# Gates of a routed layer by one 256-column matmul per token, with other portions of side work per block

## The chip, the cores and the metric

One of the cores of a Trainium2 chip runs the program. The metric is the device time of one execution in microseconds (us).

## What is computed

The reference is one layer of a decoder with 512 tokens of width 2048. Attention comes first (latent heads and sliding-window heads, and an output projection that is added to the input: `h`). What matters here is the last part, a retrieval over 16384 small experts, `h + peer(rms_norm(h))`:

```
q = (xt @ w_q).reshape(T, PEER_HEADS, 2, PEER_DQ // 2)
s = jnp.einsum('thpd,hpnd->thpn', q, sub_keys)
s_half, i_half = lax.top_k(s, PEER_TOPK)
...
top_s, pos = lax.top_k(cand, PEER_TOPK)
idx = jnp.take_along_axis(cand_idx, pos, axis=-1)
g = jax.nn.softmax(top_s, axis=-1)
...
u = expert_u[ic]
a = jnp.einsum('cd,ced->ce', xc, u)
w = (gc * jax.nn.gelu(a)).astype(xc.dtype)
return jnp.einsum('ce,ced->cd', w, expert_v[ic])
```

Each token picks 8 x 16 = 128 experts out of 128 x 128. An expert is one row of `expert_u` and one row of `expert_v`, both 16384 x 2048 float32 (134 MB each).

## The kernel before, in words

The kernel does the last part in two ways. For tokens 128 to 511 (the dense tokens, `TD` = 384) it multiplies with all experts and weights the result with a gate that is zero for experts not picked. For tokens 0 to 127 it gathers the picked rows, one row per token and slot.

**U stage.** `u_block(e)` (line 875) takes 128 experts: `u_turn` (line 862) transposes their rows on VectorE and `split` (line 116) makes a high part on ScalarE (line 117) and a low part on VectorE (line 118), three half blocks ahead of their use. TensorE then does 48 matmuls with 384 columns (lines 883 to 885). ScalarE applies the activation function (line 890), and GpSimd's queue writes the tile to `acts_d` in memory (line 891). There are 128 such blocks.

**V stage.** From line 1055 on, 16 groups of 4 column ranges load rows of `expert_v`, split them (line 118), and TensorE multiplies them (lines 191 to 193) with the weighted activations, which `w_block` (line 1033) makes on GpSimd from the activations (`wg`, from `acts_d`) and the gates (`gg`, from `gates_d`). VectorE adds the sums to the tokens' rows (line 1059).

**Side work and what orders it.** Three things are spread over these blocks by generators that give back a cost after each piece. A `Filler` (line 122) has a credit; `run(budget)` adds the budget, up to 4.0 in all, and takes pieces while the credit is above zero. The order is that of the program; the scheduler at compile time may move an instruction ahead when its engine is free and its operands are there. On each engine the order is fixed then.

- *Routing* (`route`, line 756): the top-16 searches of one projection tile, some 10 cost units each, on VectorE and GpSimd. They start in the projection before the U stage. The loop of line 990 runs U blocks with two portions of 1.4 each until no routing is left. Only then does the program queue the next two.
- *Gates* (`dense_gates`, line 899): three times 0.6 for the tables, and then 0.17 for each of 384 tokens (and 7 more steps, as sums lag 7 tokens behind). `expand` makes for a token a one-hot tile `oj` of the 128 slots' second indices (GpSimd, line 907), a one-hot tile `on` of the first (VectorE, line 909), and `oi`, that tile times the slots' weights, once with the high and once with the low part of the weights (ScalarE, line 912). `merge` multiplies `oj` with both parts of `oi`, each 128 columns, and accumulates them in one 128-column range of a PSUM bank (line 922). After four tokens the bank is full, and ScalarE copies it to `stage` (line 929). After 16 tokens ScalarE's queue writes `stage` to `gates_d` (line 932). The share per half block is 36/(124 - e), e being the number of routing blocks.
- *Gathered rows* (`gathered`, line 956): 256 steps of 2.3 units, 128 with rows of `expert_u` (a dot product on VectorE, line 973) and 128 with rows of `expert_v` (scaled and added on VectorE, line 976). Each row tile of 1.05 MB is fetched by an indirect transfer from GpSimd's queue (line 965), two steps ahead into three buffers. In the U stage each half block gives them 0.85 (line 1020), in the V stage each of the 256 steps 1.6 (line 1067). What is left then runs in a drain after the last matmul.

Of the kernel before, what the change touches and what calls it, by code (L numbers as in the profile page):

```python
# [15 lines left out]
AF = mybir.ActivationFunctionType  # L16
ALU = mybir.AluOpType
# [19 lines left out]
SG = 8  # L37
NSG = NK // SG
GT = 16
# [13 lines left out]
def block_kernel(ctx, tc, x, positions, norm1_gain, w_in, q_a_gain, w_q_b, kv_a_gain, w_kv_b, mla_q_gain,  # L53
                 mla_k_gain, swa_q_gain, swa_k_gain, swa_sinks, rel_bias_table, group_out_gain, w_out,
                 norm2_gain, peer_w_q, peer_sub_keys, peer_u, peer_v, out):
    nc = tc.nc
# [10 lines left out]
    def pool(name, bufs=1, side=None, stack=ctx, **kw):  # L67
        return stack.enter_context(tc.tile_pool(name=name, bufs=bufs, side=side, reuse_waits="tile", **kw))
# [7 lines left out]
    def acc_tile(name="acc"):  # L76
        return psum.tile([128, 512], F32, name=name, tag="acc", bufs=5)

    def tp_tile(name="tp"):
        return psum.tile([128, 512], F32, name=name, tag="tp", bufs=3)  # L80
# [35 lines left out]
    def split(hi, lo, src):  # L116
        first[0] = nc.scalar.activation(hi, src, AF.Copy)  # L117
        mark[0] = nc.vector.tensor_tensor(lo, src, hi.bitcast(F32), op=ALU.subtract)  # L118
# [33 lines left out]
    def flush(n=None):  # L152
        for _ in range(len(later) if n is None else min(n, len(later))):
            later.pop(0)()
# [486 lines left out]
    for k in range(len(units) + 3):  # L641
        if k < len(units):
# [3 lines left out]
            pieces, i, n = filling[k]  # L646
# [157 lines left out]
    def weigh(t, dst):  # L804
        e = exs[t]
        nc.scalar.activation(e, e, AF.Exp)
        z = small.tile([128, PH], F32, name="gz")
        nc.vector.tensor_reduce(z, e, axis=AX.X, op=ALU.add)
        rz = small.tile([128, PH], F32, name="grz")
        nc.vector.reciprocal(rz, z)  # L810
        nc.vector.tensor_tensor(dst.rearrange("p (h s) -> p h s", h=PH), e,
                                rz[:, :, None].to_broadcast([128, PH, TOPK]), op=ALU.mult)
# [49 lines left out]
    def u_turn(n):  # L862
        if n >= 2 * NK:
            return
        e, hf = divmod(n, 2)
        if hf == 0:
            u_load(e + 2)
        hi, lo = part_pair(n, [128, 8, 128])
        uT = up.tile([128, 8, 128], F32, name="uT")
        nc.vector.transpose(uT.rearrange("p k (b j) -> p b k j", j=32),  # L870
                            u_raw[e].rearrange("p b (k i) -> p b k i", k=KC)[:, :, hf * 8:hf * 8 + 8, :])
        split(hi, lo, uT)
        u_parts[n] = hi, lo

    def u_block(e, budget, pace=0.0):
        pa = acc_tile("pa")
        for hf in range(2):
            n = 2 * e + hf
            u_turn(n + 3)
            hi, lo = u_parts.pop(n)  # L880
            for k in range(8):
                kk = hf * 8 + k
                nc.tensor.matmul(pa[:, :TD], hi[:, k, :], xTd[0][:, kk, :], start=kk == 0, stop=False)  # L883
                nc.tensor.matmul(pa[:, :TD], hi[:, k, :], xTd[1][:, kk, :], start=False, stop=False)  # L884
                nc.tensor.matmul(pa[:, :TD], lo[:, k, :], xTd[0][:, kk, :], start=False, stop=kk == KC - 1)  # L885
            filler.run(budget)
            gatherer.run(pace)
        ga = xtp.tile([128, TD], F32, name="ga", bufs=2)
        with tc.issue_after(first[0].ins):
            nc.scalar.activation(ga, pa[:, :TD], AF.Gelu_apprx_tanh)  # L890
        nc.gpsimd.dma_start(acts_d[e], ga)
# [7 lines left out]
    def dense_gates():  # L899
        slT = [gb.tile([128, TD], F32, name=f"slT{r}") for r in range(2)]  # L900
        gT = [gb.tile([128, TD], F32R, name=f"gT{r}") for r in range(2)]
        hot, banks, stages = {}, {}, {}
        LAG = 7

        def expand(t):
            oj = gb.tile([128, NK], F32R, name="oj", bufs=LAG + 2)
            nc.gpsimd.tensor_scalar(oj, iot, slT[1][:, t:t + 1], None, op0=ALU.is_equal)  # L907
            on = gb.tile([128, NK], BF16, name="on", bufs=4)
            nc.vector.tensor_scalar(on, iotb, slT[0][:, t:t + 1], None, op0=ALU.is_equal)
            oi = gb.tile([128, 2, NK], F32R, name="oi", bufs=LAG + 2)  # L910
            for r in range(2):
                nc.scalar.activation(oi[:, r, :], on, AF.Copy, scale=gT[r][:, t:t + 1].bitcast(F32))  # L912
            hot[t] = oj, oi

        def merge(t):
            oj, oi = hot.pop(t)
            i = t % 4
            if i == 0:
                banks[t // 4] = acc_tile("gps")
            gps = banks[t // 4]  # L920
            for r in range(2):
                nc.tensor.matmul(gps[:, i * 128:(i + 1) * 128], oj, oi[:, r, :], start=r == 0, stop=r == 1)  # L922
            if i < 3:
                return
            g0, tb = t // GT, t % GT - 3
            if tb == 0:
                stages[g0] = gb.tile([128, NSG, GT, SG], F32, name="stage", bufs=2)
            stage = stages[g0]
            nc.scalar.activation(stage[:, :, tb:tb + 4, :].rearrange("p g t e -> p t g e"),
                                 gps.rearrange("p (t g e) -> p t g e", t=4, e=SG), AF.Copy)  # L930
            if tb == GT - 4:
                nc.scalar.dma_start(
                    bass.AP(tensor=gates_d.tensor, offset=gates_d.offset + g0 * GT * SG,
                            ap=[[TD * SG, 128], [128 * TD * SG, NSG], [1, GT * SG]]),
                    stage.rearrange("p g t e -> p g (t e)"))

        for t in range(1, NT):
            ts = slice((t - 1) * 128, t * 128)
            gt = gb.tile([128, SLOTS], F32, name="gt")
            weigh(t, gt)  # L940
            tp = tp_tile()
            for r in range(2):
                nc.tensor.transpose(tp[:, r * 128:(r + 1) * 128], ijs[t][:, r].rearrange("p h s -> p (h s)"), ident)
            nc.tensor.transpose(tp[:, 256:384], gt, ident)
            for r in range(2):
                nc.scalar.activation(slT[r][:, ts], tp[:, r * 128:(r + 1) * 128], AF.Copy)
            split(gT[0][:, ts], gT[1][:, ts], tp[:, 256:384])
            yield 0.6
        for t in range(TD + LAG):
            if t < TD:  # L950
                expand(t)
            if t >= LAG:
                merge(t - LAG)
            yield 0.17
# [28 lines left out]
    gatherer = Filler(paced=True)  # L983
# [5 lines left out]
    e = 0  # L989
    while filler.queue or later:  # L990
        flush(4)
        u_block(e, 1.4)
        e += 1
    filler.add(settle())
    filler.add(first_tokens())
# [7 lines left out]
    share = 36.0 / (NK - 4 - e)  # L1003
    gts, wgs, wb = {}, {}, {}

    def gate_tile(g):
        if g < NSG:
            gg = wp.tile([128, TD, SG], F32, name="gg", bufs=2)
            nc.sync.dma_start(gg, gates_d[g].rearrange("j (t e) -> j t e", e=SG))
            gts[g] = gg  # L1010

    def act_tile(e):
        if e < NK:
            wgs[e] = wp.tile([128, TD], F32, name="wg", bufs=AHEAD)
            nc.sync.dma_start(wgs[e], acts_d[e])
# [1 line left out]
    AHEAD = 5  # L1017
    wp = None
    while e < NK:
        u_block(e, share, 0.85)  # L1020
        e += 1
        if not filler.queue and wp is None:
            stg.close()
            wp = pool("wp", side="right")
            gate_tile(0)
            for i in range(AHEAD):
                act_tile(i)
# [22 lines left out]
    for g in range(NSG):  # L1050
        for c in range(4):
            acc = [acc_tile(), acc_tile(), tp_tile()]
            for i, w in enumerate(weights(v_rows[g * SG * 128:(g + 1) * SG * 128], SG, c * 512, 512, turn=4 * g + c)):
                k0 = 2 * i
                for t in range(NT - 1):
                    products(acc[t], lambda hl, kk, t: wb[g * SG + kk][hl][:, t * 128:(t + 1) * 128], t, k0, SG, w, 512)
                    if k0 == SG - 2:
                        hc = h[t + 1][:, c * 512:(c + 1) * 512]
                        mark[0] = nc.vector.tensor_tensor(hc, acc[t], hc, op=ALU.add)
                        if g == NSG - 1:  # L1060
                            nc.sync.dma_start(out[(t + 1) * 128:(t + 2) * 128, c * 512:(c + 1) * 512], hc)
                nxt = (g + 1) * SG
                if c < 3 and k0 < 4:
                    w_block(nxt + 2 * c + k0 // 2)
                if c == 3 and k0 > 2:
                    w_block(nxt + 4 + k0 // 2)
                gatherer.run(1.6)
    gatherer.drain()


# [23 lines left out]
```

## Time and profile before

| | us |
|---|---|
| median of 3 runs | 3233.54 (3232.82 to 3234.42) |
| the profiled execution, its own time | 3233.09 |
| its span, first to last instruction | 3231.4 |
| TensorE busy | 3104.4 (96%) |
| VectorE busy | 2367.1 (73%) |
| ScalarE busy | 1271.4 (39%) |
| GpSimd busy | 1248.2 (39%) |

The mean granted clock of TensorE is 0.983 of full speed. The DMA engines move 731.74 MB. The profile calls TensorE PE (its weight loads PEld), VectorE DVE, ScalarE ACT, GpSimd POOL and SyncE SP. Matmuls are pipelined: the duration of one is longer than the step to the next, so steps are read from their starts. The same holds to a smaller degree for VectorE, where the busy time of a stretch is less than the sum of durations.

### The profile page before, as it was taken

To read this page: it belongs to the slowest core of one execution; us is meant where nothing else is said; L and a number is where in the kernel's file an instruction comes from. 1 tells how busy PE (TensorE), PEld (TensorE's weight loads), DVE (VectorE), ACT (ScalarE), POOL (GpSimd) and SP (SyncE) were. 2 spreads that over 40 slices of the span, in tenths; PEclk is the share of its full clock that TensorE was granted. 3 is DMA by queue.
4 is the path that set the end of the run, shared out by engine and by line. 5 is a ranking of instruction groups with operands and counts; after the bars stand their busy time and mean duration, and the time that the engine had idled before them with its cause. 6 is when DMAs were issued, how large, how long until landed. Compare 5 with 4: busy or idle time off the path is not lost.

```text
span 3231.4 us, 43988 instructions
## 1 busy us (share of the span) xinstructions
PE 3104.4 (96%) x15802; PEld 2716.9 (84%) x15802; DVE 2367.1 (73%) x3502; ACT 1271.4 (39%) x2342; POOL 1248.2 (39%) x1260
## 2 busy tenths in 40 slices
PE   8999999989988999999999999999998999999997
PEld 6977768868788999999999999977776778887785
DVE  6436663247998567778778777788877989989896
ACT  5434452232234335566656554332222233222321
POOL 1115330001223015556566654254434445544542
PEclk9999999999999999999999999999999999999998
DMA  5422223243336668898879889998887999989896
GB/s 169 120 88 72 63 92 105 91 134 75 75 95 189 153 152 246 255 246 249 261 217 268 253 242 274 313 343 311 321 315 296 344 336 340 347 331 366 328 330 253
DMA packets 307068, 731.74 MB, mean 226 GB/s; under 512 B 24098, under 2 KB 106274, under 8 KB 269730
## 3 DMA queue, kind: packets, MB, share of 16 engines
q1 hardware_dynamic: 175394, 343.01, 33.8%
q0 software_dynamic: 45056, 293.63, 24.8%
q10 hardware_dynamic: 86400, 92.29, 10.9%
q8 instruction: 125, 2.05, 0.3%
q14 instruction: 93, 0.76, 0.1%
HBM read 666.97 MB, written 61.87 MB: 226 GB/s over the span
## 4 chain that ended last, share of the span: by engine, by line
PE 51%; DVE 13%; DMA 7%; issue 5%; POOL 2%; ACT 1%; ACTq 0%; SPq 0%; DVEq 0%; POOLq 0%
PE pa L883 10%; PE pa L885 10%; PE pa L884 10%; PE acc L192 4%; PE acc L193 4%; PE acc L191 4%; DMA wg<-acts_d 3%; DVE wlo L118 2%; PE gps L922 2%; DVE h L976 2%; PE tp L191 2%; PE tp L192 2%; PE tp L193 2%; DMA gt<-in_peer_u_dram,eidx 1%; DVE ulo L118 1%
## 5 line engine op out<-in xcount | busy, mean ns | idle before, releaser
L885 PE MATMUL pa<-xTd,wlo 128*128 128x384 f32 x1536 | 517.8, 339 | 12.5 <-DVE wlo L118 12.4
L883 PE MATMUL pa<-xTd,whi 128*128 128x384 f32 x1536 | 523.9, 341 | 0.2 <-ACT whi L117 0.2
L884 PE MATMUL pa<-xTd,whi 128*128 128x384 f32 x1536 | 519.1, 338 | 0.0
L118 DVE TENSOR_TENSOR wlo<-wraw,whi 128x1024 fp32r<-128x1024 f32 (+3 forms) x229 | 287.8, 1263 | 268.7 <-ACT whi L117 262.2
L907 POOL TENSOR_SCALAR oj<-iot,slT 128x128 fp32r<-128x128 f32 x384 | 351.4, 924 | 311.8 <-PE gps L922 310.4
L117 ACT ACTIVATE whi<-wraw 128x1024 fp32r<-128x1024 f32 (+3 forms) x229 | 232.6, 1022 | 503.6 <-PE acc L193 251.2
L973 DVE CUSTOM_DVE_ANT_0 gt<-gt,xn 128x2048 f32<-128x2048 f32 x128 | 297.6, 2325 | 53.9 <-DMA gt<-in_peer_u_dram,eidx 53.8
L976 DVE SCALAR_TENSOR_TENSOR h<-gt,w,h 128x2048 f32<-128x2048 f32 x128 | 319.7, 2497 | 18.3 <-DMA gt<-in_peer_v_dram,eidx 18.1
L118 DVE TENSOR_TENSOR wlo<-uT,whi 128x1024 fp32r<-128x1024 f32 x192 | 238.1, 1246 | 125.6 <-ACT whi L117 123.5
L192 PE MATMUL acc<-wlo,wh 128*128 128x512 f32 x768 | 306.7, 399 | 15.4 <-DVE wlo L118 15.3
L965 POOL DMA_INDIRECT gt<-in_peer_v_dram,eidx x128 | 220.2, 1720 | 256.7 <-DVE h L976 223.6
L1040 POOL TENSOR_TENSOR wg<-wg,gg 128x384 f32<-128x384 f32 x128 | 228.8, 1800 | 225.5 <-DMA wg<-acts_d 213.3
L191 PE MATMUL acc<-whi,wh 128*128 128x512 f32 x768 | 305.6, 398 | 5.0 <-ACT wh L117 5.0
L193 PE MATMUL acc<-whi,wl 128*128 128x512 f32 x768 | 305.4, 398 | 0.4 <-DVE wl L118 0.4
L885 PEld LDWEIGHTS pa<-xTd,wlo 128*128 128x128 f32 x1536 | 290.7, 189 | 13.9 <-DVE wlo L118 13.9
L883 PEld LDWEIGHTS pa<-xTd,whi 128*128 128x128 f32 x1536 | 291.3, 190 | 0.4 <-ACT whi L117 0.3
L884 PEld LDWEIGHTS pa<-xTd,whi 128*128 128x128 f32 x1536 | 291.0, 189 | 0.0
L912 ACT ACTIVATE oi<-on,gT 128x128 fp32r<-128x128 bf16 x768 | 250.6, 390 | 95.7 <-issue 24.4
L117 ACT ACTIVATE whi<-uT 128x1024 fp32r<-128x1024 f32 x192 | 200.8, 1053 | 141.0 <-PE pa L884 35.6
L965 POOL DMA_INDIRECT gt<-in_peer_u_dram,eidx x128 | 176.0, 1375 | 180.8 <-DVE a L973 158.8
L191 PE MATMUL acc<-whi,xT 128*128 128x512 f32 (+2 forms) x624 | 238.9, 383 | 4.7 <-ACT xT L117 2.3
L192 PE MATMUL acc<-wlo,xT 128*128 128x512 f32 (+2 forms) x624 | 233.5, 374 | 8.5 <-DVE wlo L118 8.4
(300 smaller groups left out, 6790.1 us busy)
## 6 DMA issues: line engine op xcount, KB each, us to landing
wraw<-in_peer_v_dram SPq DMA_DIRECT2D x86, 1024.0 KB
wraw<-in_peer_u_dram ACTq DMA_DIRECT2D x172, 256.0 KB
wraw<-in_peer_u_dram SPq DMA_DIRECT2D x172, 256.0 KB
uraw<-in_peer_v_dram SPq DMA_DIRECT2D x42, 1024.0 KB
acts_d<-ga POOLq DMA_DIRECT2D x128, 192.0 KB
gates_d<-stage ACTq DMA_DIRECT2D x24, 1024.0 KB
gg<-gates_d SPq DMA_DIRECT2D x16, 1536.0 KB
wg<-acts_d SPq DMA_DIRECT2D x128, 192.0 KB
```

What stands on the lines that cost most here:

```text
L117: first[0] = nc.scalar.activation(hi, src, AF.Copy)
L118: mark[0] = nc.vector.tensor_tensor(lo, src, hi.bitcast(F32), op=ALU.subtract)
L191: nc.tensor.matmul(o, lhs(0, kk, t), w[0][:, k, :n], start=kk == 0, stop=False)
L192: nc.tensor.matmul(o, lhs(0, kk, t), w[1][:, k, :n], start=False, stop=False)
L193: nc.tensor.matmul(o, lhs(1, kk, t), w[0][:, k, :n], start=False, stop=kk == kc - 1)
L883: nc.tensor.matmul(pa[:, :TD], hi[:, k, :], xTd[0][:, kk, :], start=kk == 0, stop=False)
L884: nc.tensor.matmul(pa[:, :TD], hi[:, k, :], xTd[1][:, kk, :], start=False, stop=False)
L885: nc.tensor.matmul(pa[:, :TD], lo[:, k, :], xTd[0][:, kk, :], start=False, stop=kk == KC - 1)
L907: nc.gpsimd.tensor_scalar(oj, iot, slT[1][:, t:t + 1], None, op0=ALU.is_equal)
L965: nc.gpsimd.indirect_dma_start(out=gt, out_offset=None, in_=u_rows if i < SLOTS else v_rows, in_offset=bass.IndirectOffsetOnAxis(ap=eidx0[ ...
L973: nc.vector.tensor_tensor_reduce(out=gt, in0=gt, in1=xn0, scale=1.0, scalar=0.0, op0=ALU.mult, op1=ALU.add, accum_out=a[:, s:s + 1])
L976: nc.vector.scalar_tensor_tensor(h[0], gt, w[:, s:s + 1], h[0], op0=ALU.mult, op1=ALU.add)
```

## The change

Each token gets one matmul of 256 columns instead of two of 128 that accumulate, so a PSUM bank holds two tokens, each with a high and a low half. ScalarE copies the high halves to `stage`, and VectorE adds the low halves to it. The portions change with it: routing 1.4 to 2.8 per half block, gathered rows 0.85 to 1.2 per half block in the U stage and 1.6 to 1.3 per step in the V stage.

```diff
         def merge(t):
             oj, oi = hot.pop(t)
-            i = t % 4
+            i = t % 2
             if i == 0:
-                banks[t // 4] = acc_tile("gps")
-            gps = banks[t // 4]
-            for r in range(2):
-                nc.tensor.matmul(gps[:, i * 128:(i + 1) * 128], oj, oi[:, r, :], start=r == 0, stop=r == 1)
-            if i < 3:
+                banks[t // 2] = acc_tile("gps")
+            gps = banks[t // 2]
+            nc.tensor.matmul(gps[:, i * 256:(i + 1) * 256], oj, oi.rearrange("p r i -> p (r i)"), start=True, stop=True)
+            if i < 1:
                 return
-            g0, tb = t // GT, t % GT - 3
+            g0, tb = t // GT, t % GT - 1
             if tb == 0:
                 stages[g0] = gb.tile([128, NSG, GT, SG], F32, name="stage", bufs=2)
             stage = stages[g0]
-            nc.scalar.activation(stage[:, :, tb:tb + 4, :].rearrange("p g t e -> p t g e"),
-                                 gps.rearrange("p (t g e) -> p t g e", t=4, e=SG), AF.Copy)
-            if tb == GT - 4:
+            sums = gps.rearrange("p (t r g e) -> p r t g e", t=2, r=2, e=SG)
+            dst = stage[:, :, tb:tb + 2, :].rearrange("p g t e -> p t g e")
+            nc.scalar.activation(dst, sums[:, 0], AF.Copy)
+            nc.vector.tensor_tensor(dst, dst, sums[:, 1], op=ALU.add)
+            if tb == GT - 2:
                 nc.scalar.dma_start(
...
         flush(4)
-        u_block(e, 1.4)
+        u_block(e, 2.8)
         e += 1
...
-        u_block(e, share, 0.85)
+        u_block(e, share, 1.2)
         e += 1
...
-                gatherer.run(1.6)
+                gatherer.run(1.3)
     gatherer.drain()
```

## Rows read from the trace of the kernel before

**Rows 1.** Busy time by stretch: us, busy (instructions) per engine, granted clock, DMA share, GB/s.

```profile
895.00:1005.00 110.00, 89.20 (x474) 85.81 (x474) 106.05 (x338) 39.67 (x53) 34.10 (x35) 0.92 0.40 100
...
1190.00:2010.00 820.00, 819.45 (x4991) 819.07 (x4991) 622.65 (x852) 485.00 (x1109) 474.37 (x528) 1.00 0.86 248
...
2090.00:2500.00 410.00, 382.61 (x1587) 301.44 (x1587) 328.35 (x315) 114.83 (x141) 178.88 (x112) 0.98 0.85 317
2500.00:3100.00 600.00, 596.48 (x2550) 477.88 (x2549) 539.02 (x418) 181.99 (x214) 303.55 (x170) 1.00 0.92 342
2860.00:2980.00 120.00, 119.05 (x510) 95.22 (x509) 114.44 (x91) 37.03 (x44) 60.85 (x37) 1.00 0.96 357
3100.00:3231.00 131.00, 110.58 (x474) 88.60 (x473) 99.22 (x77) 25.89 (x26) 36.14 (x21) 0.93 0.75 283
```

**Rows 2.** The same view of line 883 alone (TensorE, then weight loads).

```profile
895.00:1005.00 110.00, 49.60 (x139) 28.48 (x139) 0.92 0.40 100
1005.00:1190.00 185.00, 119.27 (x354) 66.80 (x354) 0.99 0.71 173
1190.00:2010.00 820.00, 479.81 (x1407) 265.15 (x1407) 1.00 0.86 248
```

**Rows 3.** The gate matmuls of line 922, ns min/median/max, first and last start.

```profile
L922 PE MATMUL gps<-oi,oj x768: 221/274/327, 1196.6 to 2004.4; 128*128 128x128 f32 x192
```

**Rows 4.** The chain that ended last: the last routing tile's reduction.

```profile
1000.18 1.22 DVE ij L791
```

**Rows 5.** Timeline of TensorE: start, us, instruction; 256, 128 (six at once), 512 columns.

```profile
116.32 0.28 PE L191 MATMUL acc<-whi,xT 128*128 128x256 f32 x1
116.44 0.28 PE L192 MATMUL acc<-wlo,xT 128*128 128x256 f32 x1
...
1512.60 0.34 PE L884 MATMUL pa<-xTd,whi 128*128 128x384 f32 x1
1512.77 0.34 PE L885 MATMUL pa<-xTd,wlo 128*128 128x384 f32 x1
1512.95 0.78 PE L922 MATMUL gps<-oi,oj 128*128 128x128 f32 x6
...
1513.79 0.34 PE L884 MATMUL pa<-xTd,uhi 128*128 128x384 f32 x1
...
2799.97 0.39 PE L191 MATMUL acc<-uhi,wh 128*128 128x512 f32 x1
...
2800.67 0.39 PE L191 MATMUL acc<-uhi,wh 128*128 128x512 f32 x1
```

**Rows 6.** Waits in the V stage: who waited for whom, us, times, longest.

```profile
PE acc L192 <- DVE wlo L118: 15.3, 11, 4.8
...
DVE gt L973 <- DMA gt<-in_peer_u_dram,eidx: 53.8, 14, 7.5
...
POOL wg L1040 <- DMA wg<-acts_d: 213.3, 57, 13.2
```

**Rows 7.** Timeline of the end: the last matmul and the last gathered row.

```profile
3210.18 0.40 PE L193 MATMUL tp<-uhi,wl 128*128 128x512 f32 x1
...
3224.09 2.35 DVE L976 SCALAR_TENSOR_TENSOR h<-gt,w,h 128x2048 f32<-128x2048 f32 x1 [0.26 <-DMA gt<-in_peer_v_dram,eidx]
```

**Rows 8.** Groups by line, 1190 to 2010: busy, mean ns, idle before.

```profile
L973 DVE CUSTOM_DVE_ANT_0 gt<-gt,xn 128x2048 f32<-128x2048 f32 x65 | 148.7, 2288 | 0.0
...
L929 ACT ACTIVATE stage<-gps 128x512 f32<-128x512 f32 x96 | 56.6, 589 | 104.3 <-PE gps L922 96.1 <-DVE uT L870 5.1 <-DVE wlo L118 1.9
```

**Rows 9.** Timeline of VectorE in the V stage: additions with an operand in PSUM.

```profile
2120.92 1.28 DVE L1059 TENSOR_TENSOR hd<-acc,hd 128x512 f32<-128x512 f32 x2
```

**Rows 10.** Waits of VectorE, 1190 to 2010.

```profile
DVE wlo L118 <- ACT whi L117: 72.6, 43, 9.3
```

**Rows 11.** The page's DMA queues: GpSimd's, with packets, MB and share.

```profile
q0 software_dynamic: 45056, 293.63, 24.8%
```

## The prediction

> **What bounds the kernel now.** I read the busy table by stretch first, then the waits inside each stretch, then the timeline for the step from one matmul to the next, and the end last. Four stretches matter.
>
> - 895 to 1005 us: the first blocks of U beside the rest of the routing. VectorE is busy 106.05 of 110 us, and TensorE gets only 139/16 = 8.7 blocks done (a block issues 16 matmuls of line 883) [rows 1, 2].
> - 1005 to 1190: 354/16 = 22.1 blocks, 8.36 us each, and no gate matmul yet: the first comes at 1196.6. The program puts the gates behind 29 blocks that carry only routing pieces, although VectorE reduces the last routing tile at 1000.18 [rows 2 to 4].
> - 1190 to 2010: 1407/16 = 87.9 blocks, 9.32 us each. TensorE never pauses (819.45 of 820 us, clock 1.00), VectorE is busy 622.65 us, 7.08 per block [rows 1, 2]. TensorE is the bound here, and each of the 768 gate matmuls lengthens the run.
> - 2090 to the end, the V stage: from 2500 to 3100 TensorE is full again, but from 2090 to 2500 it issues 1587 matmuls, at three in 0.70 us that is 370 of 410 us [rows 1, 5]: 40 us are lost, and to transfers. TensorE waits for VectorE's low parts, VectorE 53.8 us for gathered rows, GpSimd 213.3 us for the activations' tile [rows 6]. At the end the last matmul starts at 3210.18, while the last gathered row is added from 3224.09 on and the span closes at 3231.4: a tail of 21 us [rows 7].
>
> **The change, part by part.** Which block carries what follows from the tally of credits that the fillers keep. For the kernel before it gives 29 routing blocks, the tokens on 88 blocks (trace: 87.9), (128-29)*1.7/2.3 = 73 gathered rows by the end of U, 256*1.6/2.3 = 178 in V, and 5 for the drain, which fits a tail of 21 us.
>
> *Doubled routing portions.* 29 blocks of 2.8 credits become 15 of 5.6. The tokens then lie on blocks 15 to 112, 97.5 of them: 384/97.5 = 3.94 tokens a block instead of 4.37. The trace does not show routing at this pace. VectorE is 96% busy in that stretch already and its instructions stay the same, so a gain is excluded; two blocks of U pushed behind the routing would cost 17 us. I take 0, because the last piece, by the tally in block 28, runs beside block 8.7 as it is, so the tally hardly rules there; the 17 stays for the range.
>
> *One matmul of 256 columns.* Between the matmul of line 885 at 1512.77 and that of line 884 at 1513.79 lie six gate matmuls of 128 columns: 1.02 us less two steps of 8.36/48 = 0.174 leaves 0.67, so 0.112 each. The blocks say (9.32-8.36)/(768/87.9) = 0.110. A 256-column matmul steps by 0.12 [rows 2, 5]. So 768*0.110 = 84 us become 384*0.12 = 46: 38 us of TensorE saved, all on the path as long as TensorE is the bound.
>
> The Trainium skill ("TensorE: Matmul & The Clock Gate", Back-to-back issue gap) gives one matmul by itself N/2.4 + 2.5 ns, 56 ns for 128 columns and 109 for 256. By that two short ones cost what one long one costs, and the sum would have 1 us here instead of 38; the trace disagrees, with 0.110 us for the short one.
>
> *One copy of 512 elements becomes two copies of 256 and two additions.* ScalarE's copy takes 0.589 us; two shorter ones cost at most twice that, 57 us more over the stage, in 335 us of idle time (485 of 820 busy) [rows 1, 8]. VectorE gains 192 additions with one operand in PSUM. The nearest row is the addition of 512 elements from PSUM in the V stage, two in 1.28 us [rows 9]. Bounds for 256: 0.30 (somewhat under half) and 0.64 (nothing saved); I take 0.35, near the half, as both have one element per lane and step: 1.97*0.35 = 0.69 us per block. Each addition waits for ScalarE's copy, which waits for TensorE; behind it on VectorE stand transposes and low parts of the next U blocks, and the PSUM bank is held until VectorE is done. The 24 writes of the gates wait in ScalarE's queue for VectorE's addition, with the next high part behind them. These waits go into the ends of the U stage below.
>
> *Gathered rows, 0.85 to 1.2 and 1.6 to 1.3.* (128-15)*2.4/2.3 = 118 rows by the end of U, 44 more than now: 1.04 a block instead of 0.74. The other 138 go at 1.3/2.3 a step and end near step 244 of 256. Each moved row takes its product of 2.29 us on VectorE [rows 8], its issue on GpSimd's queue (busy 474 of 820 us) and 1.05 MB of transfer with it.
>
> *U stage.* TensorE per dense block: 8.36 + 3.94*0.12 = 8.83 us. VectorE: 7.08 + 0.30*2.29 + 0.69 - 0.09 (0.43 fewer one-hot rows) = 8.37, 95% of that. It reached 96% from 895 to 1005, and 95% from 2860 to 2980 with TensorE at 119.05 of 120 [rows 1]. The margin is thin, and low parts wait 72.6 us for one kind of high part even now [rows 10]. I take 9.0 us, with ends 8.83 (TensorE) and 9.3 (VectorE at 90%). U then ends at 1005 + (15-8.7)*8.36 + 97.5*9.0 + 15.5*8.36 = 1005+53+877+130 = 2065 instead of 2090: -25 us (-42 to +4).
>
> *V stage.* VectorE loses 44*2.29 = 101 of its 967 us (sum of three rows), the DMA engines 46 MB. TensorE's own work stays, so at most the 40 us and the tail come back. Of the 40 I take half, 20 (ends 0 and 35), since the first activations must still arrive. Of the tail, once the rows are done before the last matmul, its addition (0.64) and the last write remain, about 6 us by the 4.9 from the end of the last row (3226.4) to 3231.4: 15 saved. Together -35 (-15 to -50).
>
> Sum: -25 - 35 = -60 on 3233.09, the profiled execution's own time, 0.45 us under the median: 3173. All ends together: 3141 to 3239, with the 17 us.
>
> **Rivals.**
> 1. *VectorE starves TensorE in U* (the slower one). VectorE, in order, stops at an addition or a low part until ScalarE delivers. Busy only 83% while it is the bound, it takes 8.37/0.83 = 10.1 us a block: U ends at 1188+983 = 2171, +81, the whole +46: 3279. The sign turns where U loses 35 us: 937 us for 97.5 blocks, 9.61 each, VectorE at 87%. For it: the 72.6 us of waits, and 80% from 2090 to 2500 in spite of a starving TensorE. Against: most of those waits fall where VectorE is ahead, and the crowded stretches show 95%.
> 2. *Transfers bind U.* The DMA engines are busy 0.86 of 9.32 us, 8.0 per block; 0.30 rows of 1.05 MB at 293.63 MB/(0.248*3231.4 us) = 366 GB/s add 0.86 [rows 1, 11]: 8.9. At the 0.96 of the crowded V stretch a block takes 9.25: U +0, V -35, 3198. Against: the same engines move 342 GB/s in V and 248 here.
> 3. *The wide matmul saves nothing*, because only columns count: a block takes 8.36 + 3.94*0.22 = 9.23, U -2, V -35: 3196. Against: the 0.110 beside the 0.12. It is what the rule named above makes of it.
> 4. *The change doesn't move what it says*: gates and rows still start near 1190, since something other than the portions holds them. Then 88 blocks at 9.07 (-22), 102 rows in U, 9 left for the drain (V -8): 3203.
>
> **How the numbers follow.** Forecast 0.52, rivals 0.22, 0.12, 0.05, 0.09. What a measurement of this kernel can tell from no change is 0.2%, 6.5 us. Faster: 0.48 of the forecast, 0.11, 0.05 and 0.07 of rivals 2 to 4, 0.01 of rival 1: 0.72. Same: 0.09, the forecast's upper end and what lies about the turning point. Slower: 0.19, nearly all rival 1. The range starts at 3140, where every part is at its good end, and goes to 3262, VectorE at 84%; outside lie the worse half of rival 1 and a little at the bottom.
>
> **What would show it.** Right: gate matmuls 0.12 apart, the first near 1060 us; dense blocks of 8.8 to 9.3 us with VectorE about 93% busy and TensorE near full; U ending near 2065; less lost before 2500; no row after the last matmul. Wrong: TensorE waiting over 80 us for low parts inside U, VectorE waiting for ScalarE's copies of the gates, a DMA share of 1.00 in U with loads coming late, or additions of over 0.6 us.

## The result and the profile after

The changed kernel takes **3192.14 us** (median of 4 runs, 3190.16 to 3195.45), beside 3233.18 for the kernel before on the same chip: a ratio of 0.9875 [0.9858, 0.9892], 41 us less. The forecast was 3173 in a range of 3140 to 3262: faster was right, by 41 us instead of 60. The profiled execution took 3190.16 us with a span of 3188.4.

In the code after, the gate matmul is line 921, ScalarE's copy 930, VectorE's addition 931, the write of the gates 933, the dot product 974, the addition of a gathered row 977, and the addition to the tokens' rows in V 1060. The loads of `expert_u` stay at line 858.

First the busy table by stretch, as in [rows 1]: us, then busy time and instructions of PE, PEld, DVE, ACT and POOL, granted clock, DMA share, GB/s.

```profile
1066.00:1966.00 900.00, 873.07 (x5061) 868.32 (x5060) 805.85 (x1155) 513.15 (x1234) 584.17 (x574) 0.98 0.94 279
1200.00:1940.00 740.00, 719.74 (x4177) 715.84 (x4176) 663.81 (x956) 419.68 (x1011) 486.82 (x478) 0.98 0.95 282
2096.00:2500.00 404.00, 396.88 (x1676) 316.23 (x1677) 342.55 (x281) 123.25 (x149) 176.82 (x108) 0.99 0.87 325
2500.00:3100.00 600.00, 600.00 (x2573) 482.88 (x2572) 493.98 (x400) 183.78 (x214) 246.97 (x148) 1.00 0.82 304
```

The V stage is what was hoped for. From 2096 to 2500 TensorE issues 1676 matmuls, at 0.70/3 us each 391 of 404 us, so 13 us are lost where 40 were; from 2500 on it is full. VectorE and the DMA engines have less to do in the second half.

The dense blocks of U are not. TensorE pauses for 27 of the 900 us, where it paused for half a microsecond in 820 before [rows 1]. VectorE is at 805.85 of 900, which is 90%, and the DMA share is 0.94 instead of 0.86. The same view of line 883 alone gives the pace (16 such matmuls are a block):

```profile
1200.00:1940.00 740.00, 436.72 (x1288) 244.99 (x1288) 0.98 0.95 282
```

1288/16 = 80.5 blocks in 740 us are **9.19 us a block**. Counted over all gates, 1065.8 to 1966.6, it is 900.8/97.5 = 9.24. The gate matmuls (the line's instructions with ns min/median/max, first and last start), and how far apart they start, in TensorE's timeline:

```profile
L921 PE MATMUL gps<-oi,oj x384: 277/283/552, 1065.8 to 1966.6; 128*128 128x256 f32 x192
```

```profile
1244.30 0.54 PE L921 MATMUL gps<-oi,oj 128*128 128x256 f32 x3
1244.67 0.34 PE L883 MATMUL pa<-xTd,uhi 128*128 128x384 f32 x1
```

Three of them take 0.37 us until the next matmul starts: 0.123 each. So a block's work on TensorE is what the prediction said, 8.83 us, and 80.5 such blocks are 711 us: 29 of the 740 are lost. The new and changed groups (1190 to 2010; busy, mean ns, idle before) cost no more than the forecast's ends allowed:

```profile
L974 DVE CUSTOM_DVE_ANT_0 gt<-gt,xn 128x2048 f32<-128x2048 f32 x92 | 211.3, 2297 | 0.0
...
L931 DVE TENSOR_TENSOR stage<-stage,gps 128x256 f32<-128x256 f32 x164 | 67.1, 409 | 22.4 <-ACT stage L930 22.2
...
L930 ACT ACTIVATE stage<-gps 128x256 f32<-128x256 f32 x163 | 58.3, 373 | 107.5 <-PE gps L921 72.9 <-DVE uT L870 14.2 <-issue 11.5
```

And the end, in the timeline: the last gathered row is added 59 us before the last matmul, where it came 14 us after it [rows 7].

```profile
3124.55 2.35 DVE L977 SCALAR_TENSOR_TENSOR h<-gt,w,h 128x2048 f32<-128x2048 f32 x1
...
3184.03 0.40 PE L193 MATMUL tp<-uhi,wl 128*128 128x512 f32 x1
```

**Where the 29 us go.** The waits of TensorE from 1200 to 1940 (who waited for whom: us, times, longest), in the kernel after:

```profile
PE gps L921 <- ACT ga L890: 7.0, 1, 7.0
PE gps L921 <- DVE stage L931: 6.2, 3, 4.4
PE pa L883 <- ACT ga L890: 3.5, 1, 3.5
PE pa L885 <- DVE wlo L118: 2.0, 4, 0.7
```

They name ScalarE as often as VectorE. ScalarE is busy 419.68 of 740 us, so it is not overloaded; what it waits for itself is the question. In the same view "issue" means that it waited for nothing that the profile shows:

```profile
ACT oi L912 <- issue: 68.6, 9, 13.8
```

Nine stops, 68.6 us, the longest 13.8. ScalarE's timeline and that of its queue (ACTq) at the longest one:

```profile
1278.08 0.85 ACTq L858 DMA_DIRECT2D wraw<-in_peer_u_dram  x2
...
1279.99 0.39 ACTq L933 DMA_DIRECT2D gates_d<-stage  x1
...
1281.48 0.68 ACT L912 ACTIVATE oi<-on,gT 128x128 fp32r<-128x128 bf16 x2
1283.10 12.82 ACTq L858 DMA_DIRECT2D wraw<-in_peer_u_dram  x2
1295.96 0.69 ACT L912 ACTIVATE oi<-on,gT 128x128 fp32r<-128x128 bf16 x2 [13.81 <-issue]
1296.56 0.47 ACT L890 ACTIVATE ga<-pa 128x384 f32<-128x384 f32 x1
...
1297.17 0.76 PE L921 MATMUL gps<-oi,oj 128*128 128x256 f32 x2 [6.98 <-ACT ga L890]
1298.03 0.69 PE L883 MATMUL pa<-xTd,whi 128*128 128x384 f32 x1
```

This is the reading of the case. ScalarE's queue issues the gates' write, and then two loads of the next rows of `expert_u`. The issue of two loads took 0.85 us at 1278.08, before the write; of these two behind it, it takes 12.82. ScalarE starts nothing until that issue has ended, at 1295.92, so everything behind it stands too: `oi` for the next gate matmul, the activation function that frees a PSUM bank, the next high part. TensorE runs dry at 1290 and stands for 7 us. It is not a single case: all 14 issues of U loads on ScalarE's queue that took over 1.6 us in this trace are the first or the second behind a write of the gates. The next 10 us in the busy table, and TensorE's timeline before and after the pause:

```profile
1290.00:1300.00 10.00, 2.48 (x8) 1.51 (x7) 2.25 (x4) 4.04 (x10) 2.53 (x3) 0.66 1.04 324
```

```profile
1279.94 0.34 PE L883 MATMUL pa<-xTd,whi 128*128 128x384 f32 x1
1280.11 0.34 PE L884 MATMUL pa<-xTd,whi 128*128 128x384 f32 x1
...
1300.30 0.52 PE L884 MATMUL pa<-xTd,whi 128*128 128x384 f32 x1
1300.62 0.52 PE L885 MATMUL pa<-xTd,wlo 128*128 128x384 f32 x1
```

Before the pause such matmuls start 0.17 us apart, behind it 0.32, up to 1303.5: TensorE is at the lower of its two levels (1.2 GHz) for a while, and the granted clock of these 10 us is 0.66. The pauses of the 740 us sum to 20.3 (740 less 719.74). Of the other 9 us of the 29, some 7 are such slow steps: from one start to the next, 50 steps of the 740 us take about 0.32 us instead of 0.17.

The kernel before has the same stops. Its waits of ScalarE, 1200 to 1940:

```profile
ACT uhi L117 <- issue: 25.1, 7, 5.0
ACT oi L912 <- issue: 23.8, 11, 4.6
ACT whi L117 <- issue: 21.6, 7, 4.9
ACT ga L890 <- issue: 6.3, 3, 2.9
```

With one of 1.2 us these are 78.0 us, 29 times, none longer than 5.0. TensorE pauses 0.6 us in all there. So the sum of the stops alone doesn't explain the loss, and the experiments had to find what makes them count.

### The profile page after: what moved, and what is told of

It reads as the page before. It is cut to its first block, busy times and chain, and to the rows that moved or that the text cites. A ratio compares the mean times of both kernels' runs of the same rounds, so it can differ in the third digit from the quotient of the medians.

```text
span 3188.4 us, 42942 instructions
## 1 busy us (share of the span) xinstructions
PE 3074.1 (96%) x15418; PEld 2688.7 (84%) x15418; DVE 2431.3 (76%) x3694; ACT 1273.9 (40%) x2438; POOL 1275.9 (40%) x1260
## 3 DMA queue, kind: packets, MB, share of 16 engines
q0 software_dynamic: 45056, 293.63, 25.2%
q10 hardware_dynamic: 86400, 92.29, 10.6%
## 4 chain that ended last, share of the span: by engine, by line
PE 54%; DVE 15%; DMA 3%; issue 3%; ACT 1%; ACTq 1%; POOL 1%; DVEq 0%; SPq 0%; POOLq 0%
PE acc L191 8%; PE acc L193 7%; PE acc L192 7%; PE pa L885 7%; PE pa L883 7%; PE pa L884 7%; PE tp L191 4%; PE tp L193 3%; PE tp L192 3%; DVE uT L870 3%; DVE wlo L118 3%; DVE gt L974 2%; DMA wg<-acts_d 1%; DVE ulo L118 1%; ACTq L858 1%
## 5 line engine op out<-in xcount | busy, mean ns | idle before, releaser
L907 POOL TENSOR_SCALAR oj<-iot,slT 128x128 fp32r<-128x128 f32 x384 | 416.3, 1092 | 258.2 <-PE gps L921 256.7
L966 POOL DMA_INDIRECT gt<-in_peer_v_dram,eidx x128 | 198.7, 1552 | 360.8 <-DVE h L977 329.1
L883 PEld LDWEIGHTS pa<-xTd,whi 128*128 128x128 f32 x1536 | 294.7, 192 | 8.0 <-ACT ga L890 3.8
L884 PEld LDWEIGHTS pa<-xTd,whi 128*128 128x128 f32 x1536 | 294.4, 192 | 0.0
L191 PE MATMUL acc<-whi,xT 128*128 128x512 f32 (+2 forms) x624 | 237.7, 381 | 4.3 <-ACT xT L117 2.7
L193 PE MATMUL acc<-whi,xT 128*128 128x512 f32 (+2 forms) x624 | 236.2, 379 | 0.0
```

The costliest lines, as they stand in the source:

```text
L191: nc.tensor.matmul(o, lhs(0, kk, t), w[0][:, k, :n], start=kk == 0, stop=False)
L193: nc.tensor.matmul(o, lhs(1, kk, t), w[0][:, k, :n], start=False, stop=kk == kc - 1)
```

## The experiments

Three explanations are tested. **VectorE's load** (theory A in the expectations): with the additions and more gathered rows it has no reserve and TensorE starves (rival 1, milder). **The DMA side** (theory B): more is moved in U, and the issues of loads (B1) or the transfers as such (B2) come late (rival 2, in another form). **Both together** (AB): the stops on the DMA side start the loss, and VectorE without reserve can't make it up. A theory C, that the additions hold VectorE up because it waits in order, falls with e10 below: there all additions are in place and TensorE is full.

All results in one table. Ratios are to the kernel before, run on the same chip. The runs lie on several chips, where the medians of the kernel before range from 3232.1 to 3236.9, so a difference between the times of two rows holds to some 5 us. "Block", "pause" (740 less TensorE's busy time), "stops" (ScalarE's issue waits, and the longest) and the three columns behind them hold for 1200 to 1940 us; "V start" is the first matmul of V. The profiled executions give them.

| run | us | ratio [95%] | block | pause | stops (longest) | VectorE | GB/s | V start |
|---|---|---|---|---|---|---|---|---|
| before | 3233.18 | 1 | 9.34 | 0.6 | 78 (5.0) | 77% | 248 | 2089.7 |
| after | 3192.14 | 0.9875 [0.9858, 0.9892] | 9.19 | 20.3 | 72 (13.8) | 90% | 282 | 2096.7 |
| e1 wide matmul only | 3212.66 | 0.9921 [0.9904, 0.9938] | 8.98 | 5.1 | 62 (9.0) | 87% | 257 | 2058.8 |
| e2 portions only | 3204.80 | 0.9911 [0.9896, 0.9927] | 9.40 | 9.2 | 117 (11.3) | 81% | 276 | 2107.1 |
| e3 rows as before | 3204.04 | 0.9896 [0.9878, 0.9913] | 8.95 | 6.7 | 64 (7.7) | 85% | 256 | 2068.4 |
| e4 no addition | 3175.24 | 0.9816 [0.9800, 0.9831] | 9.16 | 17.7 | 122 (12.0) | 83% | 285 | 2090.3 |
| e5 loads from SyncE | 3196.99 | 0.9890 [0.9873, 0.9906] | 8.94 | 5.2 | 0 | 93% | 292 | 2094.3 |
| e6 half the U rows fetched | 3148.53 | 0.9738 [0.9719, 0.9757] | 8.94 | 7.6 | 38 (11.5) | 92% | 231 | 2064.2 |
| e7 short dot product | 3145.01 | 0.9731 [0.9712, 0.9750] | 8.84 | 2.3 | 93 (13.2) | 71% | 295 | 2059.6 |
| e8 before, loads from SyncE | 3532.30 | 1.0918 [1.0897, 1.0940] | 12.54 | 111.5 | 7 (7.0) | 58% | 179 | 2394.7 |
| e9 gates' write from SyncE | 3153.07 | 0.9738 [0.9723, 0.9753] | 8.79 | 0.3 | 9 (2.1) | 93% | 296 | 2060.7 |
| e10 gates' write from GpSimd | 3150.22 | 0.9734 [0.9721, 0.9747] | 8.78 | 0.0 | 13 (2.2) | 93% | 297 | 2059.7 |
| e11 before, write from GpSimd | 3229.85 | 0.9995 [0.9982, 1.0009] | 9.32 | 0.0 | 23 (2.9) | 77% | 247 | 2090.1 |
| e12 portions, write from GpSimd | 3189.99 | 0.9874 [0.9856, 0.9891] | 9.20 | 0.0 | 20 (1.8) | 85% | 284 | 2095.9 |

**e1: the wide matmul alone**, with the portions of before.

```diff
-        u_block(e, 2.8)
+        u_block(e, 1.4)
...
-        u_block(e, share, 1.2)
+        u_block(e, share, 0.85)
...
-                gatherer.run(1.3)
+                gatherer.run(1.6)
```

> The wide matmul with its copies and additions alone; routing 1.4, rows 0.85 and 1.6 as before. Theory A (VectorE's load sets the U stage once the matmul is cheaper): VectorE has about 7.8 us of work in a dense block, TensorE 8.36 + 4.37*0.12 = 8.9, so TensorE stays the bound, a dense block falls from 9.32 to 8.9, U loses 35 us and V stays: 3195 to 3200. Theory B (transfers set the U stage): the transfers are those of before, so the same 35 us are gained. Theory C (the additions hold up VectorE, which waits for ScalarE and TensorE in order, whatever the rest): blocks stay at 9.1 to 9.3 and the time at 3215 to 3233.

U ends 31 us earlier (2058.8), with the gates on 88 blocks as before. V takes 11 us more than before (1131.6 us from its first to its last matmul, 1120.5 before) and keeps its tail of 21 us. So U behaved and V gave a third back; where these 11 us arise was not traced.

**e2: the portions alone**, with the two short matmuls of before: the same three lines the other way, in the kernel before.

> The portions alone (2.8, 1.2, 1.3) with the two short matmuls. TensorE has 8.36 + 3.94*0.22 = 9.23 us in a dense block, VectorE 7.7. Theory A: TensorE-bound at 9.23, U ends near 2088 as before, V gains its 49 us: about 3184 to 3188, so the wide matmul would be worth nothing in the end. Theory B: the blocks take 9.3 to 9.4 by the transfers, U ends 2095 to 2105, the time is 3190 to 3200, and the DMA share of the dense blocks is 0.93 or more.

V takes 1092.5 us, as in the kernel after (1091.7): the whole gain in V belongs to the portions. U is 17 us *longer* than before. VectorE is at 81%, well below 90, and still TensorE pauses for 9.2 us, with the stops of ScalarE larger than anywhere but in e4. Its waits:

```profile
ACT whi L117 <- issue: 67.7, 13, 10.8
ACT uhi L117 <- issue: 45.9, 8, 11.3
```

**e3: the rows' portions as before** (0.85 and 1.6), the rest as after. The diff is the last two lines of e1's.

> The changed kernel with the gathered rows' portions of before (0.85 and 1.6), routing at 2.8. 84 rows in U, none left for the drain. Theory A: VectorE has 7.75 us in a dense block, TensorE 8.83 binds, U ends near 2050 (45 us sooner than in the changed kernel). Theory B says the same, as 34 MB leave the U stage. In V the rows run at the old rate, so 15 us of the tail are gained and the 40 us before 2500 stay lost: 3170 to 3180. Theory C: U ends near 2090 all the same, 3210 to 3220.

3204, not what was expected. U gains 21 us on before, V only the tail. Inside V it takes 9 us more than before (1129.7 us to the last matmul), as e1 did, although fewer rows are left for V than before (171, where it was 176); why is open. So the other portions of the rows are worth 12 us by the medians (3204.04 to 3192.14), and 7 by the ratios, whose intervals overlap.

**e4: without VectorE's addition** (the low half of the gates is left out of the result).

```diff
             nc.scalar.activation(dst, sums[:, 0], AF.Copy)
-            nc.vector.tensor_tensor(dst, dst, sums[:, 1], op=ALU.add)
```

> The changed kernel without the addition of the low halves on VectorE (that part of the gates is left out of the result). VectorE's work in a dense block falls from about 8.4 to 7.7 us, the transfers stay. Theory A and theory C: dense blocks fall from 9.3 to 8.85 to 8.9, U ends 40 us sooner, 3150 to 3155. Theory B: blocks stay at 9.2 to 9.3, time within 10 us of the changed kernel's 3192.

17 us less than after by the medians (9 by the profiled executions), but the dense block stays at 9.16 us with VectorE at 83%, and TensorE pauses for 17.7 us. The stops grow to 122 us and lie in front of the high parts themselves:

```profile
ACT uhi L117 <- issue: 68.5, 13, 11.5
ACT whi L117 <- issue: 52.5, 11, 12.0
```

So the additions' load on VectorE isn't the cause by itself.

**e6 and e7: each load on its own.** e6 fetches every second row of `expert_u` only and uses it twice; e7 takes the dot product over 128 of the 2048 columns, with every row still fetched. The dot products of the rows not fetched, and of the other columns, are left out of the result.

```diff
-            if i < 2 * SLOTS:
-                gt = fetched[i] = gp.tile([128, D], F32, name="gt", bufs=3)
+            if i < SLOTS and i % 2:
+                fetched[i] = twice[0]
+            elif i < 2 * SLOTS:
+                gt = twice[0] = fetched[i] = gp.tile([128, D], F32, name="gt", bufs=3)
```

```diff
-                nc.vector.tensor_tensor_reduce(out=gt, in0=gt, in1=xn0, scale=1.0, scalar=0.0, op0=ALU.mult,
+                nc.vector.tensor_tensor_reduce(out=gt[:, :128], in0=gt[:, :128], in1=xn0[:, :128], scale=1.0, scalar=0.0, op0=ALU.mult,
```

> The changed kernel that fetches only every second gathered row of the first table and uses each fetched tile twice (the other rows' share of the result is left out). VectorE's work is the same, 62 MB of transfers leave the U stage. Theories B1 and B2: the DMA share of the dense blocks falls from 0.95 to 0.85 or less, and U ends 25 to 40 us sooner, 3150 to 3165. Theory A: U ends within 10 us of the changed kernel's 2096.

> The changed kernel with the products of the gathered rows of the first table over 128 of 2048 columns (the rest of each product is left out). The transfers stay, VectorE's work in a dense block falls from about 8.3 to 6.3 us. Theory A: U ends 30 to 40 us sooner, 3150 to 3160. Theories B1 and B2: the stops stay, U ends within 12 us of 2096, as it did without the additions.

Each brings the time near 3150, more than 40 us below after, with some work left out. With half the fetches VectorE is at 92%, busier than after, and TensorE pauses for 7.6 us instead of 20.3: the stops are down to 38 us. With the short dot product the transfers are as dense as anywhere (295 GB/s) and the stops are there, 93 us, one of 13.2:

```profile
ACT oi L912 <- issue: 73.0, 20, 13.2
```

But VectorE at 71% makes them up, and TensorE pauses for 2.3 us. Against after, which has stops of that length in front of the same instructions, only VectorE's load is lower. So both count: the stops, and how much time VectorE has to catch up. How much is enough isn't shown: at 83% in e4, with the stops in front of the high parts, it wasn't.

**e5 and e8: the loads off ScalarE's queue**, in the kernel after (e5) and in the kernel before (e8).

```diff
-                for i, queue in ((0, nc.sync), (2, nc.scalar), (1, nc.sync), (3, nc.scalar)):
+                for i, queue in ((0, nc.sync), (2, nc.sync), (1, nc.sync), (3, nc.sync)):
```

> The changed kernel with all four quarter loads of an expert tile issued from SyncE's queue, none from ScalarE's. Same transfers, same work on every engine. Theory B1 (the DMA engines are full for some microseconds, ScalarE stands still at the issue of a load, and the high parts, gate tiles and activations behind it come late): the stop of 12.8 us at 1283 and its like go, TensorE no longer pauses, a dense block falls from 9.3 to 8.85 to 9.0, U ends 30 to 40 us sooner, 3150 to 3165. Theory B2 (the transfers as such are too many for the U stage, whoever issues them): blocks stay near 9.2 to 9.3, within 10 us of 3192. Theory A (VectorE's load): no difference either.

> The kernel before with all quarter loads issued from SyncE's queue. Its DMA share in the dense blocks is 0.86 and TensorE never pauses there, so theories A, B1 and B2 all expect no difference in U: 3225 to 3240. A gain would say that the issue from ScalarE cost time before the change too, a loss that SyncE's queue can't carry the four loads.

Mixed, and a surprise. In e5 the stops of ScalarE are gone, and the block falls to 8.94 us. But the first gate comes 9 us later (1074.7), the rest of U after the gates takes 147 us instead of 130 (16 blocks instead of 15), and in sum nothing is won. In e8 the same edit costs the kernel before 9%. SyncE's queue now waits for something that it never waited for (whole span):

```profile
SPq L858 <- DMA gates_d<-stage: 425.9, 24, 23.8
```

24 waits, as many as there are writes of the gates, with all loads behind them. The same 24 waits, 394.5 us, stand in e5, which is only 5 us longer than after, so they alone don't explain the 9%. Why a load on SyncE's queue waits until a write from ScalarE's has landed was not settled. These two say that moving the loads is the wrong way to part loads and write.

**e9 and e10: the write off ScalarE's queue**, in the kernel after: `nc.sync` in e9, `nc.gpsimd` in e10.

```diff
             if tb == GT - 2:
-                nc.scalar.dma_start(
+                nc.gpsimd.dma_start(
                     bass.AP(tensor=gates_d.tensor, offset=gates_d.offset + g0 * GT * SG,
```

> The changed kernel with the 24 writes of the gates issued from SyncE's queue; the loads stay where they are. Theory AB (ScalarE's queue holds a load's issue for 3 to 12 us behind each gates write, and VectorE, over 90% busy, can't make up for it): the long issues on ScalarE go, its dense blocks fall from 9.2 to 8.9, U ends 25 to 40 us sooner, 3150 to 3170. If the loads of SyncE then wait for the gates writes to land, as they did with all loads on SyncE, the gain is less or a loss. Theory A (VectorE's load alone): within 10 us of 3192. Theory B2 (transfers as such): within 10 us of 3192.

> The changed kernel with the 24 writes of the gates issued from GpSimd's queue. Theory AB: the stops on ScalarE go as well, and U ends 25 to 40 us sooner, 3150 to 3170, unless GpSimd, which is busy 64% of the dense stretch, takes over 10 us to issue such a write; then the one-hot tiles and gathered rows behind it come late and U ends no sooner. Theories A and B2: within 10 us of 3192.

This one edit gives **3150.22 us, 0.9734 [0.9721, 0.9747]** of before, faster than both kernels: 42 us below the change as it was made, 46 by the ratios (e9: 3153.07). The busy table of e10, all engines and line 883 alone:

```profile
1200.00:1940.00 740.00, 740.00 (x4363) 740.00 (x4362) 690.72 (x985) 435.72 (x1039) 425.25 (x503) 1.00 0.95 297
...
1200.00:1940.00 740.00, 453.02 (x1349) 253.45 (x1349) 1.00 0.95 297
```

TensorE does not pause at all, and a block takes 740/(1349/16) = 8.78 us: the 8.83 that the prediction has as TensorE's own floor. VectorE is *busier* than after (93%), and the DMA engines move *more* (297 GB/s). Neither bound the stage. The instructions of the load's line and the write's (ns min/median/max) show the price:

```profile
L858 ACTq DMA_DIRECT2D wraw<-in_peer_u_dram x172: 317/371/1308, 854.0 to 2022.7; - x172
...
L858 ACTq DMA_DIRECT2D uraw<-in_peer_u_dram x84: 317/408/2633, 869.1 to 2006.5; - x84
...
L933 POOL DMA_DIRECT2D gates_d<-stage x24: 1175/1217/1249, 1101.3 to 1920.8; - x24
```

No load's issue on ScalarE's queue takes over 2.7 us (12.26 in the kernel after). GpSimd pays 1.2 us for each of the 24 writes, 29 us in all, and it is busy for only 425.25 of the 740.

On GpSimd's queue the write is also split otherwise. The page's DMA queues (packets, MB, share) of the kernel after, and of e10 twice:

```profile
q10 hardware_dynamic: 86400, 92.29, 10.6%
...
q0 software_dynamic: 51584, 318.79, 27.2%
q10 hardware_dynamic: 36864, 67.13, 8.0%
```

A write is (86400 - 36864)/24 = 2064 packets on ScalarE's queue and (51584 - 45056)/24 = 272 on GpSimd's [rows 11]. So e10 alone would leave open whether the place or the packets count. e9 settles it: SyncE's queue moves the 2064 packets a write, its total of packets is that of after, and TensorE is as full (0.3 us of pauses, 8.79 us a block). There the loads of SyncE's own queue are held instead:

```profile
L858 SPq DMA_DIRECT2D wraw<-in_peer_u_dram x172: 311/330/4983, 868.7 to 2022.3; - x172
```

Up to 4.98 us, where the longest of these was 1.52 in the kernel after, but in this kernel SyncE only issues transfers, so no computing stands behind them.

**e11 and e12: the same edit without the wide matmul**, in the kernel before (e11) and with the portions alone (e12).

> The kernel before with the 24 writes of the gates issued from GpSimd's queue. Theory AB says that the stops of ScalarE cost nothing there, because TensorE is full and VectorE at 76% makes up for them: 3225 to 3240, no difference. If the write's place is worth 40 us by itself, whatever the rest: 3190 to 3200.

> The new portions with the two short matmuls, and the gates written from GpSimd's queue. With the stops gone TensorE binds: 8.36 + 3.94*0.22 = 9.23 us a dense block, U ends near 2088, V takes 1092: 3178 to 3190. The difference to the same kernel with the wide matmul (3150) is then what the wide matmul is worth, 30 to 38 us. If it comes out at 3155 or less, the wide matmul is worth nothing.

In the kernel before it is worth nothing, 0.9995 [0.9982, 1.0009]: its 78 us of stops cost nothing, with TensorE the bound. VectorE at 77% had reserve there, and no stop was longer than 5.0 us; which of the two saved it these runs don't part, and e7 speaks for the reserve. In the kernel with the portions it is worth 3204.80 - 3189.99 = 15 us. And e12 to e10 is the wide matmul with no stops in the way: 3189.99 - 3150.22 = **40 us** (45 by the ratios), a block 9.20 to 8.78. In the kernels as made (e2 to after) it showed 13 us.

## Why the prediction was right, and where it was off

It was right that the change makes the kernel faster, and 19 us off in how much, but not by the road it gave. U was to end 25 us sooner; it ended 7 us later (2096.7, 2089.7 before), outside its stated ends of -42 to +4 and covered only by the 17 us kept for the first gate. The whole gain is V's, 50 us where 35 were forecast. That V's 15 us beyond the forecast made good part of the miss in U is luck. By stage, against its own terms:

- **First gate:** forecast near 1060 (1005 + 53), measured 1065.8. The 8 us lie inside the 17 that the range allowed for blocks pushed behind the routing.
- **The wide matmul's price:** 0.12 us forecast, 0.123 measured, and 38 us for all of them, 40 measured in e12 to e10. Rival 3 (only columns count) falls by the same pair: at its 9.23 a block there would be no difference from e12's 9.20. The rule named in the prediction (the Trainium skill, "TensorE: Matmul & The Clock Gate", Back-to-back issue gap) gave 1 us for this; the section states it for one matmul by itself and says that it gives too little for few columns in a stream of weight loads and matmuls. The 40 us and the step of 0.110 for 128 columns agree with that limit, so the rule does not hold for these matmuls.
- **Copy and addition:** 0.409 us for the addition by its duration, between the ends 0.30 and 0.64. The copy of 256 elements took 0.373. VectorE waited 16.0 us for these copies from 1200 to 1940, which is little beside what follows.
- **The dense block, the step that failed.** "I take 9.0 us", 877 us for all gates; measured 9.24 and 901. The ends (8.83 and 9.3) held it, but the reasoning behind the middle did not. It weighed VectorE's share of 95% against what VectorE had reached before. The upper end, "VectorE at 90%", even has the measured share, yet that share was not a limit: in e10 VectorE runs at 93% under a full TensorE at 8.78 us. The prediction named the 24 writes in ScalarE's queue, but only as waiting for VectorE's addition. What it missed, and so put at nothing, is the other half: a load's issue behind such a write is held for up to 12 us, and ScalarE with it. ScalarE's waits in the trace before would have shown the stops, 78 us "<- issue", though not that they would come to count; in U I read only VectorE's [rows 10].
- **Rest of U:** 130 us forecast, 130.1 measured, the same by luck: 15.0 blocks of 8.67 us, not 15.5 of 8.36. So V starts at 2096.7 instead of 2065: 8 + 24 = 32 us late.
- **V:** -35 forecast, -50 measured. To its last matmul it gained 33 us (1120.5 to 1087.4; 20 forecast, up to 35): 27 of the 40 lost before 2500 came back, and behind 2500 TensorE is full. Whether VectorE's lighter load or that of the DMA engines gave them back was not tested. The tail went from 21.2 to 4.4 us (17; 15 forecast). Half of the 40 was too cautious.
- **Sum:** 32 late less 15 gained is 17, with 2 between the profiled execution and the median: the 19 us from 3173 to 3192.

**Rival 1** (VectorE starves TensorE, 10.1 us a block) did not come: 9.24 is short of its turning point of 9.61. It had half of the mechanism, since VectorE's load is part of what makes the stops count (e7). **Rival 2** (transfers, 9.25 us a block, 3198) has nearly the right numbers for a wrong reason: e7, e9 and e10 move 295 to 297 GB/s at 8.78 to 8.84 us a block. What it half saw is that the fetches matter: with half of them the stops fall to 38 us (e6). **Rival 4** (the order doesn't move) falls by the first gate at 1065.8.

The Trainium skill says of this choice ("DMA: Bandwidth & Descriptors", Issuing engines are not separate DMA queues) that starting transfers from several engines only saves the starting engine's time, which it calls usually small beside the transfer. Here the starting engine's time was what counted: 42 us between after and e10, from where 24 writes are started. The write's own issue is small, 0.39 us on ScalarE's queue; the loads behind it are held.

**Open:** why an issue is held behind the write (the runs show only that the write is 2064 packets on its queue, and that ScalarE's stops go when the write has another queue), and what sets how long: the longest stop grows from 5.0 us in the kernel before to 11.3 with the portions alone, but also to 9.0 in e1, with the fetches of before; the 11 and 9 us in V of e1 and e3; SyncE's waits in e5 and e8, and what makes e8 so slow.

## What to carry to other kernels

When a change takes work off the bound and puts it on an engine beside it, don't ask only whether the new load fits: ask which stalls the old reserve was hiding, and read the waits of the engines that are *not* busy, "issue" among them. In this case ScalarE, which both computes for the critical path and issues transfers, stood still whenever an issue was held; try such a write on a queue whose owner has time, as e9 and e10 did. Before judging an edit by its time, look whether what it saves is lost in such a stall: the same wide matmul was worth 13 us with the stops and 40 without.

## What the runs showed of the hardware that was not expected

- The issue of two loads on ScalarE's queue takes 0.85 us alone and up to 12.82 behind a write of 1 MB on that queue; the engine does nothing meanwhile. With the write on SyncE's queue (e9) that queue's loads are held, up to 4.98 us. On GpSimd's queue (e10) the write's own issue takes 1.2 us instead of 0.39, the write is 272 packets instead of 2064, and no load's issue takes over 2.7 us.
- With all loads of U on SyncE's queue, that queue waits for each of the 24 writes of ScalarE's to land, 425.9 us in all, and the kernel before becomes 1.0918 [1.0897, 1.0940] times as long; in the kernel after, with 394.5 us of the same waits (e5), it is 5 us.
- A matmul of 256 columns steps by 0.123 us, one of 128 by 0.110 to 0.112 [rows 5]: for these matmuls, each with a weight load of its own, a step of 128 columns costs nine tenths of one of 256.
